# A two-layer decoder trunk on one core: three more weight blocks of the down-projection by seven products instead of eight, and a final norm with its statistics over 512 columns and its instructions in another order

## The chip, the cores and the metric

The kernel runs on one core of one Trainium2 chip. A core has a matrix engine (TensorE: PE in the profile, its weight loads PEld), two engines for element-wise work (VectorE: DVE; ScalarE: ACT), GpSimd (POOL) and SyncE (SP), which here only starts transfers. Each engine works through its own list of instructions in order and waits where an instruction needs what another engine or a transfer has not delivered. The metric is the device time of one execution in microseconds (us); lower is better.

## The reference

A stream `h` of 256 tokens by 2048 channels in float32 goes through two layers. Each ends with the same gated feed-forward part (5504 inner channels) and a layer norm over the channels of every token:

```
u = h @ w_up                                  # 2048 x 11008
c = conv_b + sum_j shift(u, j) * conv_w[j]    # causal, width 3
gate, val = split(c)
ff = (silu(gate) * val) @ w_down              # 5504 x 2048
h = layer_norm(ALPHA * h + ff, ln2_g, ln2_b)  # (x - mean) * rsqrt(var + eps) * g + b
```

Layer 0 mixes tokens by causal pooling before that, layer 1 by three dilated attentions. The output is `h` after the norm of layer 1, the "final norm" of this document.

## The kernel before

**Units.** All the work of TensorE is cut into numbered units, one for a block of weights of up to 512 rows by 512 columns. For every unit the block is loaded (`raw`, three buffers, by SP), split by ACT and DVE, and multiplied. The split keeps float32 accuracy: ACT writes a rounded part `wh` (L99), DVE the rest `wl = raw - wh` (L100), and every product is three matmuls (high by high, high by low, low by high). `wh` and `wl` have four buffers each. `run_units` walks the list: before the matmuls of unit i it issues the loads up to unit i+5 and the split of unit i+3, and behind them what was put off to this unit by `later(n, ...)`. So the order of instructions on every engine is fixed by the order of the units, and each engine keeps to it.

**Down-projection.** Inner channels come in chunks q = 0 to 10 of 512 (the last of 384). A token-major group (`group_tm`) multiplies several chunks with one quarter c of the 2048 output columns. A plain unit has 24 matmuls of 512 columns (L255 to L257). A chunk named in `sevens[q]` for quarter c is done with seven products of quarter blocks in place of eight, which is two units: "a" (18 matmuls of 256 columns) and "b" (24 of them, L244 to L246). Their weights are prepared by `split_sums`: for "a" DVE forms sums inside `raw` (L120, L122, L124) and a low part (L121), for "b" two low parts (L114); the raw buffer is free only after "b". The sums of the left factor are made once for a chunk by `left_sums`. When the last seven-product chunk of a group is done, `early_post` adds what its extra bank pair `s` holds: in layer 1's last groups by five DVE instructions (L845, L846, L853, L855, L857).

**The two places of the change.** In layer 0, chunks 7 and 6 (in that order) make a group for every quarter, which alternate with the up-projection of chunks 9 and 10; chunk 6 goes by sevens in all quarters, chunk 7 in quarters 0 and 1. In layer 1 the last groups are chunks 8, 9, 10 for the four quarters, with chunk 9 by sevens in quarters 0 and 2. The last quarter is done for tokens 0 to 127 first, then for tokens 128 to 255 in two halves of 256 columns (tiles `th`), so that the norm of the first token half (`finish0`) lies under the second half's matmuls; `finish1` norms the second token half after the last matmul.

**Norm.** `tm_post` adds a group's bank to `ht`, the residual in token order, and takes `bn_stats` over every 256 columns. `finish0` and `finish1` aggregate them, take the root on ACT and the reciprocal on DVE. In `finish1` the term `b - mean*rstd*g` of quarters 0 to 2 comes from TensorE: a matmul by the identity adds `b`, and one by a diagonal tile `dg` adds the rest (L936 and L943).

Of the kernel before, what the change touches and what calls it, by code (L numbers as in the profile page):

```python
# [9 lines left out]
F32 = mybir.dt.float32  # L10
F32R = mybir.dt.float32r
I32 = mybir.dt.int32
AF = mybir.ActivationFunctionType
OP = mybir.AluOpType
# [4 lines left out]
P = 128  # L19
# [13 lines left out]
def trunk(ctx: ExitStack, tc: tile.TileContext, x, pool_w_in, pool_w_grp, pool_scale, pool_w_out,  # L33
          attn_w_q, attn_w_o, shared_w_k, shared_w_v, ffn_w_up, ffn_conv_w, ffn_conv_b, ffn_w_down,
          ln1_g, ln1_b, ln2_g, ln2_b, out):
    nc = tc.nc
    V, A, PE = nc.vector, nc.scalar, nc.tensor
# [7 lines left out]
    lnp = ctx.enter_context(tc.tile_pool(name="lnp", bufs=1))  # L45
# [5 lines left out]
    def bank(nm):  # L51
        return pair(nm)[:, 0, :]
# [82 lines left out]
    def later(n, fn):  # L135
        if n == 0:
            fn()
        else:
            pending.append([n, fn])
# [158 lines left out]
    def w4(nm):  # L298
        return lnp.tile([P, 4, T], F32, name=nm, tag="w4")
# [15 lines left out]
    H, XC, XP, ST = {}, {}, {}, {}  # L315
    vec, cvec, gbx = [], [], {}
    ident = const.tile([P, P], F32, name="ident")
# [262 lines left out]
    def ffn(lay):  # L580
# [5 lines left out]
        sevens = {q: every for q in range(8)}  # L586
        sets = {0: "C", 1: "A", 2: "B", 3: "C", 4: "A", 5: "B", 6: "A", 7: "CB"[lay], 9: "A"}
        if lay == 1:
            sevens[9] = (0, 2)
        else:  # L590
            sevens[7] = (0, 1)
        free, done = {}, {}

        def pads():
# [233 lines left out]
    def to_features(c):  # L828
        hb = hp.tile([P, 4, T], F32, name="hb", tag="h")
        hf = hb.rearrange("p m t -> p (m t)")  # L830
        V.transpose(hf.rearrange("p (m t c) -> p t m c", m=4, t=2), HT[c].rearrange("p t (m c) -> p t m c", m=4))

        def to():
            H[c] = hp.tile([P, 4, T], F32, name="h", tag="h")
            return H[c].rearrange("p m t -> p (m t)")

        moves(hf, to)
# [22 lines left out]
    def tm_post(lay, n, c):  # L860
        parts = [slice(0, 256), slice(256, 512)]
        first, last = n == 0, n == 3

        def post(t, ps, half=None):
            y = HT[c][:, t, :]
            if lay == 0 and n == 2 and t == 1:
                later(3, lambda: to_features(c))
            if half is None and first:
                V.scalar_tensor_tensor(y, y, ALPHA, ps, op0=OP.mult, op1=OP.add)
            elif half is None:  # L870
                V.tensor_tensor(y, y, ps, OP.add)
            elif first:
                V.scalar_tensor_tensor(y[:, parts[half]], y[:, parts[half]], ALPHA, ps[:, :256], op0=OP.mult, op1=OP.add)  # L873
                A.activation(y[:, parts[1 - half]], y[:, parts[1 - half]], AF.Copy, scale=ALPHA)
            else:
                V.tensor_tensor(y[:, parts[half]], y[:, parts[half]], ps[:, :256], OP.add)
            if not last:
                return
            if c == 0 and t == 0:
                ST["bn"] = lnp.tile([P, 2, 8, 6], F32, name="bn", tag="bn")  # L880
            for i in range(2) if half is None else (half,):
                V.bn_stats(ST["bn"][:, t, 2 * c + i, :], y[:, parts[i]])
            if c == 2 and t == 1:
                for nm, w in (("g", ln2_g), ("b", ln2_b)):
                    r = rawp.tile([P, 4, 512], F32, name=nm, tag="raw")
                    nc.sync.dma_start(r.rearrange("p a c -> p (a c)"), w[1:2, :].to_broadcast([P, D]))
                    ST[nm] = r
                later(2, early)
            if c == 3 and t == 0:
                finish0()  # L890
            if c == 3 and half == 1:
                finish1()

        def store(by, cc, t, c=slice(0, 512)):
            by.dma_start(out[0, t * P:(t + 1) * P, 512 * cc:512 * cc + 512][:, c], HT[cc][:, t, c])

        def early():
            for t in range(2):
                for cc in range(3):
                    z = HT[cc][:, t, :]  # L900
                    V.tensor_tensor(z, z, ST["g"][:, cc, :], OP.mult)

        def finish0():
            mv = lnp.tile([P, 6], F32, name="mv", tag="mv", bufs=2)
            V.bn_aggr(mv[:, 0:2], ST["bn"][:, 0])
            A.activation(mv[:, 2:3], mv[:, 1:2], AF.Sqrt, bias=epst)
            z = [HT[cc][:, 0, :] for cc in range(4)]
            g, b = [ST["g"][:, cc, :] for cc in range(4)], [ST["b"][:, cc, :] for cc in range(4)]  # L910
            V.scalar_tensor_tensor(z[3], z[3], mv[:, 0:1], g[3], op0=OP.subtract, op1=OP.mult)
            V.reciprocal(mv[:, 3:4], mv[:, 2:3])
            V.scalar_tensor_tensor(mv[:, 4:5], mv[:, 0:1], -1.0, mv[:, 3:4], op0=OP.mult, op1=OP.mult)
            w = lnp.tile([P, 2, 512], F32, name="w", tag="sq")
            for cc in range(2):
                A.activation(z[cc], z[cc], AF.Copy, scale=mv[:, 3:4])
                V.scalar_tensor_tensor(w[:, cc, :], g[cc], mv[:, 4:5], b[cc], op0=OP.mult, op1=OP.add)
                nc.gpsimd.dma_start(z[cc], w[:, cc, :], accum_op=OP.add)
            V.scalar_tensor_tensor(z[3], z[3], mv[:, 3:4], b[3], op0=OP.mult, op1=OP.add)
            store(nc.sync, 3, 0)  # L920
            t = w4("w2")[:, 0:2, :].rearrange("p a n -> p (a n)")
            V.scalar_tensor_tensor(t, g[2], mv[:, 4:5], b[2], op0=OP.mult, op1=OP.add)
            V.scalar_tensor_tensor(z[2], z[2], mv[:, 3:4], t, op0=OP.mult, op1=OP.add)
            for cc in (2, 0, 1):
                store(nc.sync, cc, 0)

        def finish1():
            mv = lnp.tile([P, 6], F32, name="mv", tag="mv", bufs=2)  # L930
            V.bn_aggr(mv[:, 0:2], ST["bn"][:, 1])
            z = [HT[cc][:, 1, :] for cc in range(4)]
            g, b = [ST["g"][:, cc, :] for cc in range(4)], [ST["b"][:, cc, :] for cc in range(4)]
            ps = [bank("gb") for cc in range(3)]
            for cc in range(3):
                PE.matmul(ps[cc], ident, b[cc], start=True, stop=False)  # L936
            A.activation(mv[:, 2:3], mv[:, 1:2], AF.Sqrt, bias=epst)
            V.reciprocal(mv[:, 3:4], mv[:, 2:3])
            V.scalar_tensor_tensor(mv[:, 4:5], mv[:, 0:1], -1.0, mv[:, 3:4], op0=OP.mult, op1=OP.mult)
            dg = w4("dg")[:, 0, :P]  # L940
            V.tensor_scalar(dg, ident, mv[:, 4:5], None, op0=OP.mult)
            for cc in range(3):
                PE.matmul(ps[cc], dg, g[cc], start=False, stop=True)  # L943
            V.scalar_tensor_tensor(z[3], z[3], mv[:, 0:1], g[3], op0=OP.subtract, op1=OP.mult)
            V.scalar_tensor_tensor(z[3], z[3], mv[:, 3:4], b[3], op0=OP.mult, op1=OP.add)
            store(nc.scalar, 3, 1)
            for cc in range(2):
                V.scalar_tensor_tensor(z[cc], z[cc], mv[:, 3:4], ps[cc], op0=OP.mult, op1=OP.add)
                store((nc.sync, nc.scalar)[cc], cc, 1)
            for by, c in zip((nc.sync, nc.scalar), parts):  # L950
                V.scalar_tensor_tensor(z[2][:, c], z[2][:, c], mv[:, 3:4], ps[2][:, c], op0=OP.mult, op1=OP.add)
                store(by, 2, 1, c)
        return post

    ffn(0)
    marks.append(len(units))


    scale = 1.0 / math.sqrt(P)
# [172 lines left out]
    add_last(attn_w_o[0], rows4, [lambda j=j: oq[j] for j in range(4)], True, 1, 0, after=to_tokens)  # L1132
    marks.append(len(units))
    ffn(1)
    marks.append(len(units))

# [34 lines left out]
    with tc.tile_pool(name="pool", bufs=1) as pp:  # L1171
# [5 lines left out]
        for l in range(2):  # L1177
            n = 80 if l == 0 else 64
# [95 lines left out]
```

## Time and profile before

| | |
|---|---|
| median of 3 runs | 2016.1 us (2016.05 to 2018.27) |
| span of the profiled execution | 2014.9 us; its own time is not listed apart from the runs |
| TensorE clock granted | 1.000 over the span |
| HBM read | 380.01 MB, 190 GB/s over the span |
| PE, PEld, DVE, ACT busy | 2005.8, 1810.2, 1734.9, 1269.7 us |

The page sums each engine's busy time over the span. Matmuls are pipelined and their ends are modelled, so a busy PE is not PE at its peak. Two views matter here beside the page: the timeline, with the start and length of each instruction, and the chain of waits, which goes back from the last instruction, at each step to what released it or to the instruction before it on its engine. In the chain "issue" is time in which nothing that the profile shows was waited for, and a name with q (SPq, ACTq) is the engine's sequencer.

### The profile page before, as it was taken

To read this page: it belongs to the slowest core of one execution; us is meant where nothing else is said; L and a number is where in the kernel's file an instruction comes from. 1 tells how busy PE (TensorE), PEld (TensorE's weight loads), DVE (VectorE), ACT (ScalarE), POOL (GpSimd) and SP (SyncE) were. 2 spreads that over 40 slices of the span, in tenths; PEclk is the share of its full clock that TensorE was granted. 3 is DMA by queue.
4 is the path that set the end of the run, shared out by engine and by line. 5 is a ranking of instruction groups with operands and counts; after the bars stand their busy time and mean duration, and the time that the engine had idled before them with its cause. 6 is when DMAs were issued, how large, how long until landed. Compare 5 with 4: busy or idle time off the path is not lost.

```text
span 2014.9 us, 31474 instructions
## 1 busy us (share of the span) xinstructions
PE 2005.8 (100%) x12760; PEld 1810.2 (90%) x12760; DVE 1734.9 (86%) x1831; ACT 1269.7 (63%) x1551; POOL 93.0 (5%) x153
## 2 busy tenths in 40 slices
PE   9999999999999999999999999999999999999999
PEld 8898988999899988889888988998899989989987
DVE  6868887999899899879896878787899899989899
ACT  6454686767766676657554445487766677667673
POOL 2000000000000000000001021000000000000000
PEclk9999999999999999999999999999999999999999
DMA  8565466666666757885465656557666756666765
GB/s 260 204 208 186 163 212 192 181 221 223 198 198 200 239 179 229 232 230 186 155 220 172 210 172 202 187 188 211 166 224 200 224 186 222 209 211 186 213 208 185
DMA packets 271297, 407.77 MB, mean 202 GB/s; under 512 B 74430, under 2 KB 85588, under 8 KB 270896
## 3 DMA queue, kind: packets, MB, share of 16 engines
q1 hardware_dynamic: 259488, 388.93, 58.8%
q0 software_dynamic: 11232, 16.18, 5.4%
q8 instruction: 100, 1.64, 0.3%
q10 hardware_dynamic: 432, 0.66, 0.1%
q14 instruction: 45, 0.37, 0.1%
HBM read 380.01 MB, written 2.10 MB: 190 GB/s over the span
## 4 chain that ended last, share of the span: by engine, by line
PE 88%; DVE 7%; ACT 2%; DMA 2%; issue 1%; SPq 0%; DVEq 0%; ACTq 0%
PE acc L180 41%; PE acc L181 21%; PE s L244 3%; PE s L246 3%; PE s L245 3%; PE acc L184 2%; PE acc L185 2%; PE acc L183 2%; PE t L246 2%; PE t L244 2%; PE t L245 2%; DVE wl L100 2%; ACT wh L99 1%; DVE wl L114 1%; DVE wl L121 1%
## 5 line engine op out<-in xcount | busy, mean ns | idle before, releaser
L180 PE MATMUL acc<-xc,wh 128*128 128x512 f32 x3264 | 1151.6, 396 | 0.0
L181 PE MATMUL acc<-xc,wl 128*128 128x256 f32 x3264 | 916.2, 281 | 0.8 <-DVE wl L100 0.8
L100 DVE TENSOR_TENSOR wl<-raw,wh 128x2048 fp32r<-128x2048 f32 (+2 forms) x304 | 654.8, 2162 | 171.0 <-ACT wh L99 163.3
L180 PEld LDWEIGHTS acc<-xc,wh 128*128 128x128 f32 x3264 | 616.1, 189 | 142.8 <-issue 0.4
L99 ACT CAST wh<-raw 128x2048 fp32r<-128x2048 f32 (+2 forms) x304 | 546.6, 1805 | 170.8 <-PE acc L180 65.7
L181 PEld LDWEIGHTS acc<-xc,wl 128*128 128x128 f32 x3264 | 615.2, 188 | 1.3 <-DVE wl L100 1.2
L113 ACT CAST wh<-raw 128x1024 fp32r<-128x1024 f32 x144 | 150.7, 1052 | 202.8 <-DVE raw L122 175.5
L114 DVE TENSOR_TENSOR wl<-raw,wh 128x1024 fp32r<-128x1024 f32 x144 | 171.8, 1221 | 11.2 <-ACT wh L113 11.2
L121 DVE TENSOR_TENSOR wl<-raw,wh 128x1536 fp32r<-128x1536 f32 x72 | 126.2, 1753 | 6.3 <-ACT wh L119 5.3
L119 ACT CAST wh<-raw 128x1536 fp32r<-128x1536 f32 x72 | 106.4, 1477 | 36.6 <-PE acc L180 26.5
L287 POOL DMA_DIRECT2D ht<-w x48 | 41.3, 1015 | 1446.4 <-DVE ht L873 720.9
L244 PE MATMUL t<-wh,g 128*128 128x256 f32 x376 | 105.8, 281 | 0.0
L246 PE MATMUL t<-wh,g 128*128 128x256 f32 x376 | 105.7, 281 | 0.0
L245 PE MATMUL t<-wl,g 128*128 128x256 f32 x376 | 105.5, 281 | 0.0
L616 ACT ACTIVATE c<-u,cv 128x256 f32<-128x256 f32 x172 | 89.5, 593 | 23.2 <-DVE f L678 16.5
L246 PE MATMUL s<-wh,xs 128*128 128x256 f32 x344 | 96.1, 279 | 0.0
L244 PE MATMUL s<-wh,xs 128*128 128x256 f32 x344 | 95.9, 279 | 0.0
L245 PE MATMUL s<-wl,xs 128*128 128x256 f32 x344 | 95.9, 279 | 0.0
L124 DVE TENSOR_TENSOR raw<-raw 128x1024 f32<-128x1024 f32 x72 | 88.2, 1225 | 2.4
L621 ACT ACTIVATE a<-u,cv 128x256 f32<-128x256 f32 x172 | 73.5, 500 | 11.9 <-DVE g L688 11.9
L607 ACT COPY u<-acc 128x512 f32<-128x512 f32 x84 | 46.8, 572 | 46.1 <-PE acc L181 45.9
L621 ACT ACTIVATE u<-u,cv 128x256 f32<-128x256 f32 x172 | 73.4, 500 | 0.0
(338 smaller groups left out, 3443.1 us busy)
## 6 DMA issues: line engine op xcount, KB each, us to landing
raw<-in_ffn_w_up_dram SPq DMA_DIRECT2D x160, 1024.0 KB, 5.2
raw<-in_ffn_w_down_dram SPq DMA_DIRECT2D x80, 1024.0 KB, 5.1
raw<-in_pool_w_out_dram SPq DMA_DIRECT2D x16, 1024.0 KB, 5.0
raw<-in_shared_w_k_dram SPq DMA_DIRECT2D x16, 1024.0 KB, 5.2
raw<-in_attn_w_q_dram SPq DMA_DIRECT2D x16, 1024.0 KB, 5.3
raw<-in_shared_w_v_dram SPq DMA_DIRECT2D x16, 1024.0 KB, 5.4
raw<-in_attn_w_o_dram SPq DMA_DIRECT2D x16, 1024.0 KB, 5.2
ht<-w POOLq DMA_DIRECT2D x50, 256.0 KB, 4.8
```

The lines of the kernel that those rows point to most:

```text
L99: A.copy(wh[i][:, s], r[:, s])
L100: V.tensor_tensor(wl[i][:, s], r[:, s], wh[i][:, s].bitcast(F32), OP.subtract)
L113: A.copy(h[:, :, n], r[:, :, n])
L114: V.tensor_tensor(l[:, :, n], r[:, :, n], h[:, :, n].bitcast(F32), OP.subtract)
L119: A.copy(hs, rs)
L121: V.tensor_tensor(ls, rs, hs.bitcast(F32), OP.subtract)
L180: PE.matmul(ps[m].ap, h[:, k, c], q[:, k, :, :T], start=st, stop=False)
L181: PE.matmul(ps[m][:, :T], l[:, k, c], q[:, k, 0, :T], start=False, stop=sp)
L244: PE.matmul(to, xh, h[:, k, n], start=opens and kk == 0, stop=False)
L245: PE.matmul(to, xh, l[:, k, n], start=False, stop=False)
L246: PE.matmul(to, xl, h[:, k, n], start=False, stop=ends and kk == 1)
L621: A.activation(to[:, m, :], u[:, m, i:i + T], AF.Copy, scale=cv[:, i, j:j + 1])
```

## The change

- `sevens`: in layer 0 chunk 7 goes by seven products in all four quarters (quarters 2 and 3 are new); in layer 1 chunk 9 in quarters 0, 1 and 2 (1 is new). Where all four quarters of a chunk go by sevens, `left_sums` puts the fourth sum into unused columns of the chunk's own tile instead of the tiles `xs3S` and `xs3Q`.
- Statistics are taken over 512 columns where the whole row is there; the halves of the last quarter of the second token half stay apart. The tile `bn` and the aggregations shrink with it.
- The last part of `finish0` (quarter 2 and three stores) becomes `rest`, which is called after the statistics of the first half of the last quarter.
- In `finish1` half of the centring of quarter 3 stands ahead of the reciprocal, and `dg` is made by ACT.

The short description of the change also speaks of low parts of sums in halves; the diff has no further edit of that kind.

```diff
@@ ffn
         sevens = {q: every for q in range(8)}
         sets = {0: "C", 1: "A", 2: "B", 3: "C", 4: "A", 5: "B", 6: "A", 7: "CB"[lay], 9: "A"}
         if lay == 1:
-            sevens[9] = (0, 2)
-        else:
-            sevens[7] = (0, 1)
+            sevens[9] = (0, 1, 2)
@@ tm_post
-                ST["bn"] = lnp.tile([P, 2, 8, 6], F32, name="bn", tag="bn")
-            for i in range(2) if half is None else (half,):
-                V.bn_stats(ST["bn"][:, t, 2 * c + i, :], y[:, parts[i]])
+                ST["bn"] = lnp.tile([P, 2, 5, 6], F32, name="bn", tag="bn")
+            if half is None:
+                V.bn_stats(ST["bn"][:, t, c, :], y)
+            else:
+                V.bn_stats(ST["bn"][:, t, 3 + half, :], y[:, parts[half]])
...
             if c == 3 and t == 0:
-                finish0()
+                ST["rest"] = finish0()
+            if c == 3 and half == 0:
+                ST["rest"]()
@@ finish0
-            V.bn_aggr(mv[:, 0:2], ST["bn"][:, 0])
+            V.bn_aggr(mv[:, 0:2], ST["bn"][:, 0, :4])
...
             store(nc.sync, 3, 0)
-            t = w4("w2")[:, 0:2, :].rearrange("p a n -> p (a n)")
-            V.scalar_tensor_tensor(t, g[2], mv[:, 4:5], b[2], op0=OP.mult, op1=OP.add)
-            V.scalar_tensor_tensor(z[2], z[2], mv[:, 3:4], t, op0=OP.mult, op1=OP.add)
-            for cc in (2, 0, 1):
-                store(nc.sync, cc, 0)
+            def rest():
+                t = w4("w2")[:, 0:2, :].rearrange("p a n -> p (a n)")
+                V.scalar_tensor_tensor(t, g[2], mv[:, 4:5], b[2], op0=OP.mult, op1=OP.add)
+                V.scalar_tensor_tensor(z[2], z[2], mv[:, 3:4], t, op0=OP.mult, op1=OP.add)
+                for cc in (2, 0, 1):
+                    store(nc.sync, cc, 0)
+            return rest
@@ finish1
             A.activation(mv[:, 2:3], mv[:, 1:2], AF.Sqrt, bias=epst)
+            def centred(c):
+                V.scalar_tensor_tensor(z[3][:, c], z[3][:, c], mv[:, 0:1], g[3][:, c], op0=OP.subtract, op1=OP.mult)
+            centred(parts[0])
             V.reciprocal(mv[:, 3:4], mv[:, 2:3])
             V.scalar_tensor_tensor(mv[:, 4:5], mv[:, 0:1], -1.0, mv[:, 3:4], op0=OP.mult, op1=OP.mult)
             dg = w4("dg")[:, 0, :P]
-            V.tensor_scalar(dg, ident, mv[:, 4:5], None, op0=OP.mult)
+            A.activation(dg, ident, AF.Copy, scale=mv[:, 4:5])
             for cc in range(3):
                 PE.matmul(ps[cc], dg, g[cc], start=False, stop=True)
-            V.scalar_tensor_tensor(z[3], z[3], mv[:, 0:1], g[3], op0=OP.subtract, op1=OP.mult)
+            centred(parts[1])
```

What this moves is seen in the order of the built programs (names carry buffer numbers; sizes are partitions by elements of the output). First DVE in layer 1's last groups, from the last low part of the gate product (L305) on; `w` and `s` are `early_post` of quarter 0, the last row the split of chunk 8 in quarter 2. Before:

```order
L305 TENSOR_TENSOR g<-c,g 128x3x256
L100 TENSOR_TENSOR wl_18401<-raw_18325,wh_18400 128x2048
L845 TENSOR_TENSOR w<-w,s 128x256
L846 TENSOR_TENSOR w<-w,s 128x256
L853 TENSOR_TENSOR ht<-ht,w 128x512
L855 TENSOR_TENSOR ht<-ht,w 128x512
L857 TENSOR_TENSOR ht<-ht,s 128x2x256
L100 TENSOR_TENSOR wl_18438<-raw_18371,wh_18437 128x1536
L100 TENSOR_TENSOR wl_18467<-raw_18398,wh_18466 128x2048
```

Where one split of chunk 9 for quarter 1 stood, six instructions stand now, four ahead of `early_post` and two behind it, in the same place of the changed kernel:

```order
L305 TENSOR_TENSOR g<-c,g 128x3x256
L120 TENSOR_TENSOR raw_18377<-raw_18377 128x2x256
L121 TENSOR_TENSOR wl_18451<-raw_18377,wh_18450 128x2x768
L122 TENSOR_TENSOR raw_18377<-raw_18377 128x2x256
L124 TENSOR_TENSOR raw_18377<-raw_18377 128x4x256
L843 TENSOR_TENSOR w<-w,s 128x256
L844 TENSOR_TENSOR w<-w,s 128x256
L851 TENSOR_TENSOR ht<-ht,w 128x512
L853 TENSOR_TENSOR ht<-ht,w 128x512
L855 TENSOR_TENSOR ht<-ht,s 128x2x256
L114 TENSOR_TENSOR wl_18491<-raw_18377,wh_18490 128x4x256 x2
L100 TENSOR_TENSOR wl_18525<-raw_18448,wh_18524 128x1536
```

A second `early_post`, that of quarter 1, follows some ten rows later, ahead of the last two low parts of quarter 2; before, none stood there:

```order
L120 TENSOR_TENSOR raw_18522<-raw_18522 128x2x256
L121 TENSOR_TENSOR wl_18576<-raw_18522,wh_18575 128x2x768
L122 TENSOR_TENSOR raw_18522<-raw_18522 128x2x256
L124 TENSOR_TENSOR raw_18522<-raw_18522 128x4x256
L843 TENSOR_TENSOR w<-w,s 128x256
L844 TENSOR_TENSOR w<-w,s 128x256
L851 TENSOR_TENSOR ht<-ht,w 128x512
L853 TENSOR_TENSOR ht<-ht,w 128x512
L855 TENSOR_TENSOR ht<-ht,s 128x2x256
L114 TENSOR_TENSOR wl_18616<-raw_18522,wh_18615 128x4x256 x2
```

So the last low parts of quarter 2 now stand five instructions further back.

The third place is ACT in layer 0, from the split of chunk 7 for quarter 3 to the weights of the value half of chunk 10 (`c<-u,cv` is a step of the convolution). Before:

```order
L99 CAST wh_7888<-raw_7811 128x2048
L119 CAST wh_7918<-raw_7856 128x2x768
L113 CAST wh_7953<-raw_7856 128x4x256 x2
L607 COPY u<-acc 128x2x256
L607 COPY u<-acc 128x256
L99 CAST wh_7998<-raw_7916 128x1536
L616 ACTIVATE c<-u,cv_583 128x256 x3
```

The same place in the changed kernel:

```order
L119 CAST wh_7913<-raw_7842 128x2x768
L113 CAST wh_7944<-raw_7842 128x4x256 x2
L119 CAST wh_7978<-raw_7911 128x2x768
L605 COPY u<-acc 128x2x256
L605 COPY u<-acc 128x256
L113 CAST wh_8024<-raw_7911 128x4x256 x2
L614 ACTIVATE c<-u,cv_583 128x256 x3
L99 CAST wh_8061<-raw_7976 128x1536
```

The rounded parts for "b" of chunk 6 have moved behind the two copies, and the cast for the first value unit behind the three convolution steps.

## The prediction, made before the changed kernel was run

> **What bounds the kernel now.** I read the page first, then the chain of waits, then the busy time in stretches.
>
> ```profile
> span 2014.9 us, 31474 instructions
> PE 2005.8 (100%) x12760; PEld 1810.2 (90%) x12760; DVE 1734.9 (86%) x1831; ACT 1269.7 (63%) x1551; POOL 93.0 (5%) x153
> PE 88%; DVE 7%; ACT 2%; DMA 2%; issue 1%; SPq 0%; DVEq 0%; ACTq 0%
> ```
>
> Over the whole span PE carries the chain, with 88% of it, and has next to no idle time. The chain is not the same everywhere, though. Layer 1's last groups, where the third new unit lies, read so, engine by engine:
>
> ```profile
> core 0: us, PE busy (x) PEld busy (x) DVE busy (x) ACT busy (x) POOL busy (x), PEclk, DMA share, GB/s
> 1960.00:1985.00 25.00, 25.00 (x130) 21.09 (x129) 24.58 (x28) 12.14 (x10) 0.00 (x0) 1.00 0.62 209
> 1985.00:2005.00 20.00, 20.00 (x120) 17.65 (x120) 19.29 (x32) 5.04 (x7) 1.72 (x2) 1.00 0.41 144
> ```
>
> DVE is busy for 24.58 of 25.00 us and then 19.29 of 20.00. It has no room left there, and the chain of waits of the same place runs through it:
>
> ```profile
> 1960.13 0.06 DVE wl L100
> ...
> 1962.34 0.42 DVE w L845
> ...
> 1965.05 1.19 DVE wl L100
> ...
> 1969.00 0.61 DVE ht L871
> ...
> 1969.63 0.75 DVE bn L882 x2
> ...
> 1971.76 0.59 DVE raw L120
> ...
> 1976.01 2.36 DVE wl L114 x2
> 1978.37 0.02 issue
> 1978.38 4.93 DMA raw<-in_ffn_w_down_dram
> ...
> 1983.42 1.92 ACT wh L99
> ...
> 1985.36 2.29 DVE wl L100
> ...
> 2003.35 0.68 DVE w L922
> ...
> 2004.80 0.34 DVE ht L876
> ...
> 2005.60 0.33 DVE ht L876
> ...
> 2006.41 0.38 DVE mv L931
> ```
>
> From 1960.13 to 2006.41 it is DVE after DVE, with one load (of chunk 9 for the last quarter, whose raw buffer is free only at 1978.37) in between; DVE worked on other things meanwhile. PE is no wait in it: its last product for the tokens ends where the row below starts, and DVE begins the first of the two last additions at 2004.80, the second at 2005.60.
>
> ```profile
> 2004.75 0.59 PE L936 MATMUL gb<-b,ident 128*128 128x512 f32 x1
> ```
>
> So PE and DVE arrive at the end together, and in these 45 us a microsecond taken from PE is worth nothing unless DVE is relieved too, while one laid on DVE is paid in full.
>
> **PE's gain.** Four PE rows of layer 0, the first matmul of the pair of chunks 7 and 6 and the first behind it, for quarter 1 (both by sevens) and quarter 2 (chunk 7 plain):
>
> ```profile
> 773.58 0.28 PE L244 MATMUL s<-wh,g 128*128 128x256 f32 x1
> ...
> 783.39 0.39 PE L180 MATMUL acc<-xc,wh 128*128 128x512 f32 x1
> ...
> 805.88 0.40 PE L255 MATMUL t<-wh,g 128*128 128x512 f32 x1
> ...
> 816.41 0.39 PE L180 MATMUL acc<-xc,wh 128*128 128x512 f32 x1
> ```
>
> With chunk 7 plain the pair takes 816.41 - 805.88 = 10.53 us, by sevens 783.39 - 773.58 = 9.81. A unit by sevens saves 0.72 us of PE, three 2.2.
> [...]
>
> **DVE's price of one such unit.** In the chain, "a" takes 1971.76 to 1976.01 and "b" to 1978.37: 6.61 us. The plain split it replaces takes 1960.13 to 1962.34: 2.21. That is 4.40 us more DVE per unit. In layer 1, quarter 1 gets its own `early_post` too, five instructions, as quarter 0's from 1962.34 to 1965.05: 2.71.
>
> **Layer 0, two units.** PE gains 1.44. DVE gets 8.80 more and spares two half-width additions (0.61 - 0.34 each). What covers that:
>
> ```profile
> 813.21 1.76 DVE L100 TENSOR_TENSOR wl<-raw,wh 128x1536 fp32r<-128x1536 f32 x1 [3.38 <-DMA h<-hb]
> 832.26 2.32 DVE L114 TENSOR_TENSOR wl<-raw,wh 128x1024 fp32r<-128x1024 f32 x2
> 840.98 0.28 PE L244 MATMUL s<-wh,xs 128*128 128x256 f32 x1
> ```
>
> For quarter 2 the idle 3.38 us ahead of 813.21 take most of the 4.40. Some 1.0 us of backlog, less 0.27 for quarter 2's addition, goes on to quarter 3, which brings its own 4.40. There, chunk 6's "b" parts end at 832.26 + 2.32 = 834.58 and PE wants them at 840.98: 6.4 us of slack. In the changed kernel PE comes 1.44 earlier and DVE some 5.1 later, so the slack is -0.2, about zero; PE can start on the first of the two low parts, and I take a stall of 0.3 for what this sum leaves open. Behind it ACT's order counts: the cast for the next unit stands behind the two "b" casts and three convolution steps, where it stood ahead of the steps, and I take 0.5 for that. Net for layer 0: -1.44 + 0.8 = -0.6, bounds -1.4 (no stall) and +1.0 (a backlog of 2.4 us, all of it stalled). The loads that follow wait longer for their raw buffers (chunk 7's is held until its "b" is split), and SP's queue puts one load behind eleven small `h<-hb` transfers. The slack of a load here is about the three units of its look-ahead, so I cost that at nothing; if it is late, ACT's cast is the next to wait. The gain reaches the end, because after this stage the chain is PE's until layer 1's end.
>
> **Layer 1, one unit.** DVE: +4.40 + 2.71 = 7.1. PE's 0.72 less is worth nothing, since DVE ends last. DVE's first new instruction needs only the raw block, not ACT's cast that ended at 1960.1, so it starts some 0.15 earlier. Nothing stands between to absorb the rest: DVE's only wait (for the load above, then ACT's 1.92) moves along, since that load starts when quarter 2's "b" is split, before and after. PE in its turn has to wait. With the changed list laid out on these durations, it waits some 1.2 us for "b" of quarter 1, 0.6 for chunk 8 and 0.6 for "b" of quarter 2, and 2.6 for chunk 10 behind the second `early_post`: 5.0 in all. It ends 5.0 - 0.7 = 4.3 later than before, DVE's last addition comes some 6.5 later, so the products then lie there about 3 us before DVE asks for them.
>
> **Statistics.** Two rows of 256 take 0.75 together. One over 512 is not in the trace. Nearest are additions: 0.61 at 512 against 0.34 at 256, so 512 costs 0.07 less than twice 256. I take 0.68 for 0.75. Seven such pairs change (both token halves of quarters 0 to 2, one of quarter 3); those of quarter 1 lie ahead of the wait for the load and only lengthen it. Five count: 0.35, and 0.05 for the smaller aggregation. Bounds: 0 (as two halves) to 5 x 0.34 = 1.7 (a 512 as cheap as a 256). A pair dearer than now is excluded by the additions.
>
> **`rest` moved.** The same instructions (0.68 and 0.75) stand between the two halves' additions instead of ahead of both. DVE comes late to both halves, so the sum stays: nothing. Were DVE early, they would fill its wait for the second half, up to 1.4. SP's three stores go out later, but two of them wait for POOL's additions anyway and none is last.
>
> **`finish1`.**
>
> ```profile
> 2006.82 0.30 ACT mv L937
> ...
> 2007.15 0.17 DVE mv L938
> ...
> 2007.54 0.30 DVE dg L941
> ...
> 2007.88 2.86 PE gb L943 x6
> ...
> 2010.76 0.48 DVE ht L951
> ```
>
> After the aggregation DVE waits 0.35 us for the root; half a centring (0.48 by the last row, 256 columns with the same form) goes there and pushes the reciprocal back by 0.05 to 0.15. `dg` by ACT instead of DVE: its nearest rows are the root at one column, 0.30, and this of the page, at 256:
>
> ```profile
> L621 ACT ACTIVATE a<-u,cv 128x256 f32<-128x256 f32 x172 | 73.5, 500 | 11.9 <-DVE g L688 11.9
> ```
>
> For 128 columns I take 0.40 where DVE took 0.30. What DVE saves behind it, half a centring and `dg`, lies under the 2.86 us of PE that decide when the last rows start. So +0.15, bounds 0 and +0.4.
>
> **Sum** against the profiled execution: 2014.9 - 0.6 (layer 0) + 7.1 - 0.15 - 0.4 (layer 1 and statistics) + 0.15 (`finish1`) = 2021.0. The median of the runs, 2016.1, lies 1.2 over the span; I take that as constant: 2022.2, or +0.30%. Anything within 0.2% (4.0 us) can't be told from no change.
>
> **Rivals.**
>
> A: *PE decides.* By the page, PE and its weight loads (100% and 90%) stand over DVE's 86%. If DVE's work in the last groups can slip behind PE's, each unit gives its 0.72, -2.2, and `rest` fills a gap, up to 0.4 more: 2016.1 - 2.6 = 2013.5, not slower. It decides if DVE has at least 7 us of slack there; the 24.58 of 25.00 speaks against it, and the chain, in which no PE row stands between 1960.13 and 2007.88.
> [...]
>
> B: *The gains all go to their good ends:* no stall in layer 0 (-1.4) and a 512-column statistic as cheap as a 256 one (-1.7), against 7.1 - 0.15 - 0.05 (aggregation) + 0.15 (`finish1`): +3.95, so 2020.1, at the edge of no change.
>
> C: *Backlog in layer 0.* DVE's and ACT's lists there were near full, and if ACT's cast comes later than I worked out, quarters 2 and 3 stall for 2.5 us and more together: +1.0 in place of -0.6, and another microsecond of waits for raw buffers: 2022.2 + 2.6 = 2024.8. It speaks for it that the slack is about zero by my sum, against it that quarters 0 and 1 run the same sequence without loss, though between longer units.
>
> That the change does not do what it says is excluded by the order of the built programs, which holds the new units, the single statistics and the moved `rest`.
>
> **How the numbers follow.** My forecast 0.64 (its own range 2020.4 to 2024), C 0.10, B or something like it 0.11, A 0.11, and 0.04 for something else that makes it faster by a way I don't see. Forecast and C are slower by over 0.2%, save a tenth of the forecast at its lower edge: 0.68. A, B and the rest of the forecast's edge lie within: 0.28. Faster by over 0.2% would need -4.0, more than all gains that I find together: the 0.04. The range leaves out A and the last of C: 2017.5 to 2024.5.
>
> **What the profile of the changed kernel would show.** PE: quarters 2 and 3 of layer 0 at about 9.8 and 10.6 us instead of 10.53, with a wait on DVE or ACT at the second. In the last groups, waits of PE for `wl` (L114 and L100) of 1 to 3 us each, which were none before; DVE without a gap; the aggregation of `finish1` 6 us later against PE's arrival in layer 1's last groups. A statistic over 512 columns at 0.6 to 0.7 us a piece. `dg` by ACT at about 0.4. I am wrong if PE shows no such waits, or if DVE turns out to have idle time between 1960 and the end.

## The result, and the profile after

The changed kernel takes 2026.58 us (median of 5 runs, 2024.44 to 2030.28), the kernel before 2017.74 us beside it: a ratio of 1.0051 with a 95% interval [1.0040, 1.0062], some 10 us slower (the two medians are 8.8 us apart, within that interval). The forecast was 2022.2 with a range up to 2024.5. Single executions of one kernel lie several us apart here, so what follows rests on such ratios with their intervals, and profiles are read for places, not for totals. The profiled execution took 2024.44 us, at a span of 2022.7.

The page of the changed kernel, its span, engines and chain:

```profile
span 2022.7 us, 31610 instructions
PE 2006.8 (99%) x12814; PEld 1812.5 (90%) x12814; DVE 1748.9 (86%) x1844; ACT 1275.5 (63%) x1559; POOL 93.1 (5%) x153
PE 46%; DVE 8%; ACT 2%; DMA 2%; issue 1%; POOL 0%; SPq 0%; DVEq 0%; ACTq 0%; POOLq 0%
```

PE's busy time is about that of before (2005.8), DVE's is 14 us more. Busy time by engine in layer 1's last groups (columns as in the prediction):

```profile
1961.00:1986.00 25.00, 24.73 (x140) 21.13 (x139) 24.66 (x29) 12.76 (x12) 0.00 (x0) 1.00 0.45 158
1986.00:2013.00 27.00, 24.77 (x139) 21.18 (x139) 26.00 (x37) 6.57 (x7) 1.72 (x2) 0.94 0.46 156
```

DVE is as full as it was (24.66 of 25.00, then 26.00 of 27.00), PE has gaps now, and the granted clock is 0.94 in the second stretch. The chain of waits of the changed kernel at the same place, from the first new instruction to the last norm:

```profile
1961.38 0.60 DVE raw L120
...
1965.55 0.42 DVE w L843
...
1969.39 1.22 DVE wl L114
...
1981.37 0.34 DVE w L843
...
1990.67 6.05 DMA raw<-in_ffn_w_down_dram
...
2014.16 0.30 DVE mv L937
...
2014.48 0.48 DVE ht L946
...
2015.33 0.41 ACT dg L952
...
2015.79 2.86 PE gb L954 x6
```

The sums of the new unit (L120 to L114) and two `early_post` (L843, at 1965.55 and 1981.37) stand in the chain of DVE, and the last aggregation comes at 2014.16 in place of 2006.41. From the first instruction of the new unit it is 2014.16 - 1961.38 = 52.78 us; before, from the split that it replaces, 2006.41 - 1960.13 = 46.28: +6.50. Of the span's 7.8 us, 1.25 are there already when DVE enters these groups (1961.38 against 1960.13).

Those come from layer 0, behind which PE stays about 3 us late (3.17 at the matmul below, 2.97 at 1955). The first matmul of layer 0's norm, before and after, is the plainest sign of it (timeline of PE; in brackets the idle time ahead of the instruction and what ended it):

```profile
887.36 0.28 PE L384 MATMUL shift<-S,ones 128*128 128x256 f32 x1
```

```profile
890.53 0.36 PE L384 MATMUL shift<-S,ones 128*128 128x256 f32 x1 [2.61 <-DVE S L367]
```

It is 3.17 us late, and 2.61 of it are a wait for DVE that the kernel before does not have. In the profiles of four kernels run below that leave layer 0's units as they were, this matmul lies between 0.14 us early and 0.51 late, so single profiles can be read here to about half a us. I had forecast PE 0.6 us early there. What makes DVE late begins some 50 us earlier. Here is the timeline of SP's queue before, and then of the changed kernel (raw blocks by L89, small transfers `h<-hb` between them):

```profile
824.75 2.57 SPq L89 DMA_DIRECT2D raw<-in_ffn_w_up_dram  x2
832.37 3.86 SPq L821 DMA_DIRECT2D h<-hb  x6
836.32 0.55 SPq L89 DMA_DIRECT2D raw<-in_ffn_w_up_dram  x1
836.91 3.20 SPq L821 DMA_DIRECT2D h<-hb  x5
840.21 0.56 SPq L89 DMA_DIRECT2D raw<-in_ffn_w_up_dram  x1
```

```profile
825.00 0.37 SPq L89 DMA_DIRECT2D raw<-in_ffn_w_up_dram  x1
833.66 3.86 SPq L819 DMA_DIRECT2D h<-hb  x6
837.62 0.55 SPq L89 DMA_DIRECT2D raw<-in_ffn_w_up_dram  x1
838.21 3.20 SPq L819 DMA_DIRECT2D h<-hb  x5
841.50 0.55 SPq L89 DMA_DIRECT2D raw<-in_ffn_w_up_dram  x1
842.09 4.22 SPq L819 DMA_DIRECT2D h<-hb  x5
846.41 0.55 SPq L89 DMA_DIRECT2D raw<-in_ffn_w_up_dram  x1
```

Before, two up-projection blocks go out ahead of the first six small transfers, in the changed kernel one; the second leaves at 837.62 instead of about 827, the third at 841.50 instead of 836.32, the fourth at 846.41 instead of 840.21. The look-ahead of `run_units` counts units, and a plain unit that becomes "a" and "b" is two: the same number of units ahead now reaches one block less far, while the small transfers stay where they were.

The queue is not the whole of it: a load also waits for its raw buffer. The third block takes the buffer of chunk 6 in quarter 3, which is free when DVE has made the last low part for "b": 832.26 + 2.32 = 834.58 before, and in the changed kernel the last row of that work ends at 839.85 + 1.22 = 841.07 (timeline of DVE):

```profile
839.85 1.22 DVE L114 TENSOR_TENSOR wl<-raw,wh 128x1024 fp32r<-128x1024 f32 x1
```

So the queue holds the third block for 0.43 us only. The second, whose buffer is free at 832.47, it holds for 5.15, but no engine waits for that one. For the third block ACT does wait, where it did not before (timeline of ACT, before and after):

```profile
841.69 1.47 ACT L99 CAST wh<-raw 128x1536 fp32r<-128x1536 f32 x1
```

```profile
847.62 1.48 ACT L99 CAST wh<-raw 128x1536 fp32r<-128x1536 f32 x1 [2.03 <-DMA raw<-in_ffn_w_up_dram]
```

and DVE's list goes back with it (timeline of DVE, before and after):

```profile
844.87 1.22 DVE L305 TENSOR_TENSOR g<-c,g 128x1024 fp32r<-128x1024 f32 x1
...
885.23 0.42 DVE L367 TENSOR_TENSOR S<-fold 128x256 fp32r<-128x256 f32 x1
```

```profile
850.80 1.22 DVE L305 TENSOR_TENSOR g<-c,g 128x1024 fp32r<-128x1024 f32 x1
...
889.96 0.42 DVE L367 TENSOR_TENSOR S<-fold 128x256 fp32r<-128x256 f32 x1
```

The gate product is 5.93 us late, as is ACT's cast, and the sum `S` 4.73, and for `S` PE waits.

### The profile page after: what moved, and what is told of

It reads as the page before. It is cut to its first block, busy times and chain, and to the rows that moved or that the text cites. A ratio compares the mean times of both kernels' runs of the same rounds, so it can differ in the third digit from the quotient of the medians.

```text
span 2022.7 us, 31610 instructions
## 1 busy us (share of the span) xinstructions
PE 2006.8 (99%) x12814; PEld 1812.5 (90%) x12814; DVE 1748.9 (86%) x1844; ACT 1275.5 (63%) x1559; POOL 93.1 (5%) x153
## 4 chain that ended last, share of the span: by engine, by line
PE 46%; DVE 8%; ACT 2%; DMA 2%; issue 1%; POOL 0%; SPq 0%; DVEq 0%; ACTq 0%; POOLq 0%
PE acc L180 21%; PE acc L181 11%; DVE wl L100 2%; PE s L246 2%; PE s L244 2%; PE s L245 2%; PE t L246 1%; PE t L245 1%; PE t L244 1%; ACT wh L99 1%; PE acc L184 1%; PE acc L185 1%; PE acc L183 1%; DMA raw<-in_ffn_w_down_dram 1%; DVE wl L121 1%
## 5 line engine op out<-in xcount | busy, mean ns | idle before, releaser
L100 DVE TENSOR_TENSOR wl<-raw,wh 128x2048 fp32r<-128x2048 f32 (+2 forms) x301 | 647.9, 2160 | 162.8 <-ACT wh L99 161.4
L99 ACT CAST wh<-raw 128x2048 fp32r<-128x2048 f32 (+2 forms) x301 | 540.8, 1804 | 167.1 <-PE acc L180 66.7
L113 ACT CAST wh<-raw 128x1024 fp32r<-128x1024 f32 x150 | 156.8, 1052 | 206.6 <-DVE raw L122 186.9
L114 DVE TENSOR_TENSOR wl<-raw,wh 128x1024 fp32r<-128x1024 f32 x150 | 179.0, 1221 | 11.3 <-ACT wh L113 11.3
L121 DVE TENSOR_TENSOR wl<-raw,wh 128x1536 fp32r<-128x1536 f32 x75 | 131.4, 1752 | 7.2 <-ACT wh L119 6.0
L246 PE MATMUL t<-wh,g 128*128 128x256 f32 x396 | 111.4, 281 | 0.0
L244 PE MATMUL t<-wh,g 128*128 128x256 f32 x396 | 111.3, 281 | 0.0
L245 PE MATMUL t<-wl,g 128*128 128x256 f32 x396 | 111.2, 281 | 0.0
L245 PE MATMUL s<-wl,xs 128*128 128x256 f32 x362 | 101.0, 279 | 0.3 <-DVE wl L114 0.3
L246 PE MATMUL s<-wh,xs 128*128 128x256 f32 x362 | 101.0, 279 | 0.0
L244 PE MATMUL s<-wh,xs 128*128 128x256 f32 x362 | 100.9, 279 | 0.0
L245 PEld LDWEIGHTS t<-wl,g 128*128 128x128 f32 x396 | 74.7, 189 | 0.0
```

Of the source, the lines that this page charges most:

```text
L99: A.copy(wh[i][:, s], r[:, s])
L100: V.tensor_tensor(wl[i][:, s], r[:, s], wh[i][:, s].bitcast(F32), OP.subtract)
L113: A.copy(h[:, :, n], r[:, :, n])
L114: V.tensor_tensor(l[:, :, n], r[:, :, n], h[:, :, n].bitcast(F32), OP.subtract)
L121: V.tensor_tensor(ls, rs, hs.bitcast(F32), OP.subtract)
L244: PE.matmul(to, xh, h[:, k, n], start=opens and kk == 0, stop=False)
```

## The experiments

**The parts alone.** Each part of the change was put into the kernel before by itself. Layer 0:

```diff
-        else:
-            sevens[7] = (0, 1)
```

> Layer 0's two units alone. The prediction's step: -0.6 us against before. The account from the trace of the changed kernel: the loads of the last up-projection weights go out behind the small h transfers, the load ring then runs late, PE waits 2.5 to 3 us at the shift matmul near 888 us, and some 1.8 us of that is caught up before layer 1's last groups: +1 to +1.6 us at the end. [...]

1.0020 [1.0011, 1.0028], 2020.48 against 2016.62: 4.0 us slower. The theory with the cost in layer 0 holds, though it cost more than the 1 to 1.6 us expected; my own term of -0.6 does not. Layer 1:

```diff
-            sevens[9] = (0, 2)
+            sevens[9] = (0, 1, 2)
```

> Layer 1's unit alone (chunk 9 by sevens in quarters 0, 1, 2). If DVE decides in the last groups: +6.8 to +7.1 us of span (4.40 for the split, 2.71 for early_post, none of the statistics' saving), with a wait of PE of 2.5 us or more for the low part of chunk 10 in quarter 2, and half-clock stretches behind it, so runs spread by some us. If PE decides: -0.7 us.

1.0039 [1.0026, 1.0052], +7.9 us where 6.8 to 7.1 were expected; the last aggregation comes at 2014.12, 7.7 us after that of the kernel before. The norm (everything else in the diff):

> The norm alone (statistics over 512 columns, rest, half centring, dg by ACT), weight units as before. With 0.60 us in place of 0.75 per pair, five of seven pairs on the way: about -0.6 us; aggregations -0.15; finish1 +0.15: -0.4 to -0.7 us. The prediction's step: -0.25. If the norm's part were free of effect: 0.

0.9999 [0.9990, 1.0008]: nothing that can be told. In its profile the chain of the last groups is PE's, so what the norm spares on DVE shortens nothing there. The parts add to 4.0 + 7.9 - 0.2 = 11.7 us; together they cost 10.3. That PE's lateness from layer 0 in part lies under DVE's longer chain in layer 1 (of its 2.97 us at 1955 only 1.25 are seen where DVE enters) would explain the difference, which is no larger than the intervals.

**What in layer 1.** The new unit without the `early_post` of its quarter, which leaves that quarter's extra sums out of the result:

```diff
+            if c == 1 and not by_dma:
+                return
```

> Layer 1's unit alone, with early_post of quarter 1 left out: its five DVE instructions and one ACT copy are not issued and what its bank pair holds is not added. If DVE decides: 2.71 us less than with it, +5.0 us against before (+4.5 to +5.3). If PE decides: the same as with it, +7.7.

1.0027 [1.0018, 1.0037], 2021.63. The aggregation comes at 2011.89, 2.23 us ahead of that with the five instructions. Counted from the first new instruction (1959.79 with them, 1960.29 without) to the aggregation it is 54.33 and 51.60 us, where it was 46.28. So the five instructions cost 2.73, and their rows take 2.71. The split costs 5.32, more than the 4.40 of its rows. The rest is a wait that the prediction did not have: DVE stands 0.80 us (0.90 with the five instructions) before "a" of quarter 2, for a load that goes out only when "b" of quarter 1 frees its raw buffer. In the chain of waits of layer 1's unit alone:

```profile
1967.81 1.23 DVE wl L114
...
1969.06 6.55 DMA raw<-in_ffn_w_down_dram
...
1975.71 1.49 ACT wh L119
...
1977.22 1.77 DVE wl L121
```

Both pieces of DVE's work are paid in full, each separately: that is shown. The wait is not in the profile of the whole changed kernel, where the same count is 52.78 with the statistics' saving in it. The profiled execution without the five instructions shows one thing more (chain of waits, and granted clock in a stretch):

```profile
2013.36 5.50 PE gb L945 x6
```

```profile
2013.00:2018.50 5.50, 5.14 (x6) 1.85 (x6) 3.19 (x5) 0.00 (x0) 0.00 (x0) 0.50 0.65 225
```

The same six matmuls that take 2.86 us above take 5.50 at a granted clock of 0.50.

**What in layer 0.** First the order on SP: with the two units, the loads of the units around the change go out one unit earlier, which restores what stood ahead of the small transfers.

```diff
-        while state["loaded"] < min(len(units), i + LD_AHEAD + 1):
+        while state["loaded"] < min(len(units), i + LD_AHEAD + 1 + (172 <= i < 190)):
```

> Layer 0's two units, with loads issued one unit earlier between units 172 and 189, so that each goes out ahead of the same h transfers as in the kernel before. If the queue's order is what made the load ring late: the wait at the shift matmul goes, and the time is -0.5 to -1.4 us against before. If DVE's and ACT's backlog alone made it: +1 to +1.6 us as without it.

1.0010 [1.0001, 1.0019]: half of the loss is gone by the ratios, whose intervals overlap, and PE's wait at the shift matmul is 1.9 in place of 2.6. Neither expectation fits. In its profile two blocks stand ahead of the first small transfers again, but the third leaves only at 840.69, and the gate product is still 4.23 us late. One of the two units alone:

```diff
-            sevens[7] = (0, 1)
+            sevens[7] = (0, 1, 2)
```

> Layer 0 with chunk 7 by sevens in quarters 0, 1 and 2, so one new unit, in quarter 2, ahead of which DVE had 3.4 us of idle time. If the loss in layer 0 comes from the backlog that quarter 3 hands on: no wait at the shift matmul beyond that of before, and -0.7 us (-1 to 0). If any new unit there upsets the load ring: +1 us or more, with a wait of 1 us or more at the shift matmul.

1.0011 [1.0002, 1.0019]: with the first unit about half of the loss is there, and in its profile a wait of 1.3 us at the shift matmul. So it is not only the second unit's lack of slack, on which the prediction had spent its care. The same with the norm:

> The norm's part and the one unit of layer 0 in quarter 2, none of the others: the two parts that should not cost. -0.7 (unit) - 0.2 (norm): -0.9 us (-1.3 to 0). If the unit in quarter 2 upsets the load ring: +1 us.

1.0008 [0.9999, 1.0017]; no gain.

**The clock.** In the profile of layer 0's units alone the granted clock halves behind the wait. Three us of that kernel, and the same three of the kernel before:

```profile
893.50:896.50 3.00, 3.00 (x11) 2.52 (x11) 2.88 (x3) 0.39 (x1) 1.90 (x2) 0.50 0.67 125
```

```profile
893.50:896.50 3.00, 3.00 (x19) 2.63 (x18) 2.73 (x5) 3.00 (x6) 0.00 (x0) 1.00 1.19 207
```

11 matmuls instead of 19 in the same 3 us: PE is 4.38 us late at the shift matmul and 6.00 behind that stretch. To see whether this is the loss, twelve matmuls by the identity were put ahead of the shift matmul, so that PE is busy while it waits:

```diff
+        if not first and lay == 0:
+            for i in range(12):
+                PE.matmul(ps[:, :P], ident, ident, start=True, stop=True)
```

> Layer 0's two units, and twelve matmuls of the identity by itself (some 2.4 us by the transposes' 0.2 us each) written to the shift bank right ahead of the shift matmul, where PE waited 2.9 us. If a half-clock stretch of 3.41 us follows PE's waiting and costs time: the clock stays at 1.000 there, the jump of 1.6 us behind the shift matmul goes, and the time is +0.5 to +1.5 us against before, with runs closer together. If the stretch costs nothing, or has nothing to do with the waiting: +3.5 to +4 us as without the filling, and more if the filling itself delays the shift matmul.

1.0035 [1.0022, 1.0049], slower than without the filling, though the clock is 1.000 in four of five runs. In the profile no half-clock stretch follows (granted clock 1.000), and the shift matmul is 2.15 us late all the same. The filling itself hardly holds it up: `S` ends at 889.21 there and the matmul starts at 889.52. Keeping the clock up does not bring the time back; the stretch was a price on top, not the cause. What the filled kernel loses beyond that lies elsewhere. A second profile of it:

> The kernel with layer 0's two units and 12 fillers ahead of the shift matmul once more, for a profile of one of its longer executions (22 to 24 us over 2000 at a granted clock of 1.0, in three of five). Theory 1 (a load lands late somewhere behind layer 0, in single executions): the PE offset against before is about +2.2 at the shift matmul as in the first profile and jumps by 3 to 6 us at one later wait on a DMA. Theory 2 (the loss in layer 0 itself varies): the offset at the shift matmul is already 5 to 8 us. If the execution is a short one (span below 2019), it tells nothing.

2025.39 us, span 2023.6, clock 1.000. At the shift matmul PE is 3.35 us late, between the two theories; the rest comes later, in five waits of this kind (waits of PE from there to 1860):

```profile
PE acc L181 <- DVE wl L100: 5.0, 5, 1.7
```

PE loses 1.2 us between 1500 and 1860 in the first profile of the filled kernel and 5.9 in the second; where those late steps begin, in which load, I did not find. The two units alone, once more:

> Layer 0's two units alone once more, for a second profile. Theory 1 (the length of the wait for the shift matmul varies little, 4.4 us in the first profile, and the half-clock stretch behind it comes or does not come): offset at the shift matmul 3.5 to 5, and the end offset is 0 to 1 us more without the stretch and 1.5 more with it. Theory 2 (the loss in layer 0 itself varies from execution to execution, between 0 and 8 us): the offset at the shift matmul differs from 4.4 by more than 1.5.

2019.78 us. The shift matmul is 2.12 us late, 2.3 less than in the first profile, so the loss in layer 0 does vary from execution to execution, and a half-clock stretch follows again (granted clock 0.50 from 890.00 to 893.00, PE 3.72 late behind it). Both theories had a part of it.

Where the two executions part can be seen. The load of chunk 7 for quarter 3 lands 9.2 us after its issue in the first (at 826.23) and 7.5 in the second (824.35). DVE begins the sums of that chunk at 826.25 and 824.93, and PE waits 1.66 and 0.56 us for the last low part for "b" of chunk 6 in quarter 3 (at 841.44 and 840.07). Behind this the two are 1.36 us apart, of the 2.26 at the shift matmul. In the changed kernel the load took 7.9 us, and PE did not wait there.

**The cause in layer 0.** If the blocks are late because they stand behind small transfers, it should help to take those off the queue. The two units, with `h<-hb` issued by POOL:

```diff
-    def moves(fr, to):
+    def moves(fr, to, by=nc.sync):
...
-                nc.sync.dma_start(dst[0][32 * b:32 * b + 32, a], fr[32 * a:32 * a + 32, b])
+                by.dma_start(dst[0][32 * b:32 * b + 32, a], fr[32 * a:32 * a + 32, b])
...
-        moves(hf, to)
+        moves(hf, to, nc.gpsimd)
```

> Layer 0's two units alone, and the 64 transfers h<-hb of the kernel (32 KB each) go by POOL's queue in place of SP's, where they stood between the loads. Theory 1 (the loads go out late behind these transfers on SP's queue, half of the loss): as with the loads one unit earlier, about +2 us against before, the shift matmul of layer 0 (887.36 in before) late by 1 to 1.5 us in place of 4.4. Theory 2 (the raw buffers come free late, so that the order of SP does not matter): +4 as in the run with the two units alone, the shift matmul late by 4. Theory 3 (POOL's own transfers are slower to issue, so that h comes late to the convolution): later than +4, with waits on DMA h<-hb.

1.0002 [0.9993, 1.0011], 2017.52 against 2016.85. The loss is gone within the noise, which is more than theory 1 had expected. Its loads and its shift matmul (timelines of SP and PE):

```profile
824.45 0.37 SPq L89 DMA_DIRECT2D raw<-in_ffn_w_up_dram  x1
831.05 0.37 SPq L89 DMA_DIRECT2D raw<-in_ffn_w_up_dram  x1
840.00 0.37 SPq L89 DMA_DIRECT2D raw<-in_ffn_w_up_dram  x1
842.53 0.37 SPq L89 DMA_DIRECT2D raw<-in_ffn_w_up_dram  x1
```

```profile
887.04 0.36 PE L384 MATMUL shift<-S,ones 128*128 128x256 f32 x1 [0.89 <-DVE S L367]
```

The second block leaves at 831.05 instead of the changed kernel's 837.62, the fourth at 842.53 instead of 846.41, and PE waits 0.89 us. The third still leaves at 840.00: there it waits for its raw buffer and not for the queue. The gate product is therefore still 4.02 us late, but `S` only 1.24, where it was 4.73: without the transfers the lateness is caught up on the way. The control, the kernel before with the same move:

> The kernel before with only the transfers h<-hb on POOL's queue in place of SP's, as a control for the run above. Theory 1: these transfers are slack in the kernel before, PE decides there: within 0.5 us of before. Rival: POOL issues 64 transfers more slowly than SP and h comes late: +1 us or more, with PE or DVE waiting on h<-hb behind 805 us.

1.0004 [0.9995, 1.0013]: for the kernel before these transfers make no difference. So it is the two together, shown by the runs with neither, either and both: the units are harmless without the transfers on the queue, and the transfers are harmless without the units. By which way the transfers do it is not shown. They hold loads back on the queue, and without them the loads issued from 820 to 862 land 5.5 us after their issue in the median, where it was 7.1 in the changed kernel (5.2 and 7.9 for that of chunk 7 in quarter 3; the longest 9.9 and 8.3); these two were not tried apart.

**Together.** The whole change with the transfers on POOL's queue, and the same without layer 1's unit:

> The whole changed kernel with only the transfers h<-hb on POOL's queue in place of SP's. Theory 1 (the miss of the prediction is these transfers ahead of layer 0's loads, and what is left is layer 1's unit on DVE): 2016.9 + 7.9 - 0.3 = 2024.5 at the most and 2022 at the least; against the changed kernel as it is 2 to 4 us less, the shift matmul of layer 0 within 0.7 us of before in place of 3.2 late. Theory 2 (the parts do not add, so that layer 1's waiting covers what layer 0 wins): within 1 us of the changed kernel as it is, 2026.

> The changed kernel without layer 1's new unit (chunk 9 by sevens in quarters 0 and 2, as before), and with the transfers h<-hb on POOL's queue: the best version that the runs point to. Theory 1: layer 0's two units at no loss (ratio 1.0002 alone) and the norm's -0.2 us: 2016.5 to 2017, the same as before, since what PE gains by the two units is waited for again at the shift matmul. Theory 2 (the gain of 1.4 us of PE reaches the end once the loads are in time): 2015.3, 1.5 us faster.

The first takes 1.0034 [1.0021, 1.0048], about 2024 on the scale of theory 1, between its ends, and some 3.5 us less than the changed kernel as it is (1.0051; the intervals overlap a little). Its shift matmul is not within 0.7 us, though:

```profile
889.13 0.36 PE L384 MATMUL shift<-S,ones 128*128 128x256 f32 x1 [1.80 <-DVE S L367]
```

1.77 us late, with a half-clock stretch behind it: the next matmuls of 512 columns take 0.58 and 0.63 us, where those ahead of it take 0.40 and those in the changed kernel's stretch at 1991.72 take 0.63. The second is 1.0001 [0.9992, 1.0010], theory 1's "the same as before", with the same wait of 1.8 us. No version with these units that was run is faster than the kernel before; in the profiles PE waits at the shift matmul for about what the two units gain.

## Why the prediction was right or wrong

**What bounds the kernel** was read rightly: the last groups belong to DVE, and both pieces of DVE work put there cost at least their rows' time. DVE has no gap above 0.55 us there in the changed kernel.

**Layer 1** was right in size: 7.1 - 0.4 = 6.7 in the sum from the new unit's start to the aggregation, 6.50 measured. That it comes so near is in part luck: alone, the unit costs 8.05 by the same count, with DVE's wait of 0.90 for a load that the prediction left out. PE's products for the norm start later by 2011.82 - 2004.75 = 7.07 us, 2.97 of it brought along from layer 0, so 4.1 for the 4.3 worked out; but the waits lie otherwise than I had laid them out. PE's waits in the changed kernel, from 1955 to 2016:

```profile
PE t L256 <- DVE wl L100: 2.2, 1, 2.2
...
PE s L245 <- DVE wl L114: 0.3, 1, 0.3
```

The one for chunk 10 is there (2.6 forecast), and of the 0.6 for "b" of quarter 2 half; those of 1.2 for "b" of quarter 1 and 0.6 for chunk 8 are not. The waits add to 2.5 us for the 5.0 forecast, and the half-clock stretch behind the wait for chunk 10 adds some 1.6: that PE's lateness agrees is luck.

**Statistics and `finish1`** were about right and too small to matter. All 512-wide statistics of the changed kernel, by line:

```profile
L880 DVE BATCH_NORM_STATS2 bn<-ht 128x6 f32<-128x512 f32 x7 | 4.9, 695 | 0.2
```

0.70 where I took 0.68. `dg` by ACT takes 0.41 (0.40 taken), and from the aggregation to the products it is 2015.79 - 2014.16 = 1.63 us where it was 2007.88 - 2006.41 = 1.47: +0.16 for +0.15. `rest` cost nothing that shows.

**Layer 0** is the step that failed: -0.6 forecast, +4.0 measured. In the changed kernel's profile it is not the stall I worked out: the pairs of quarters 2 and 3 take 9.90 and 10.05 us (about 9.8 and 10.6 forecast), a wait of 0.45 follows (I had taken 0.5 for ACT's order), and at the start of the last groups of layer 0, behind both new units, PE was 0.31 us early. With layer 0's units alone the stall at "b" of quarter 3 is there too, 1.66 and 0.56 us in two profiles where I took 0.3, so that term was too small in some executions. What failed above all is the sentence after it: that a load's slack was "about the three units of its look-ahead, so I cost that at nothing". I had seen the block behind eleven small transfers and the buffers held longer, and named ACT's cast as next to wait; I did not work out that a look-ahead of units is a shorter one when a unit is split in two, nor that the third block's buffer comes free 6.49 us later (841.07 for 834.58), nor follow a block that leaves 5.18 us late through cast, DVE and the shift matmul some 50 us on. Taking the transfers off the queue gives back (1.0020 - 1.0002) x 2016.9 = 3.6 of the 4.0 us.

**Rival C** was nearest (2024.8, with a backlog of DVE and ACT in layer 0). Its stalls of 2.5 us in quarters 2 and 3 did not come in the changed kernel; its "another microsecond of waits for raw buffers" points at the part that did, though not at the transfers. A is out by layer 1 alone (+7.9). B is out by the statistics, 0.70 us a piece over 512 columns where B had them at the 0.42 of 256, and by layer 0.

**Time over span.** I added 1.2 us, the median of the runs over a span of another execution. Time less span is about 1.8 us in every run listed here with both. The forecast span of 2021.0 stands against 2022.7 in the profile, 1.7 us off; the rest of the miss of 4.4 is that 0.6 and a median 2.1 us above the profiled execution.

**What stays open**: how much of the loss in layer 0 is the order on the queue and how much the later landing; why one load lands 7.5 us after its issue in one execution and 9.2 in another; why two kernels with the transfers moved still wait 1.8 us at the shift matmul and a third 0.9; and where the filled kernel's later steps in layer 1 come from. More raw buffers would test how much of the rest is the buffers' part; that was not tried.

## What to carry to other kernels

Where loads are issued a fixed number of steps ahead, a change that splits a step shortens the look-ahead for everything behind it: list what each queue holds ahead of each load and when the load's buffer comes free, before and after, and follow the first late load to the engine that ends the stage. Where small transfers stand between large loads, another queue for them is worth a run: here it gave back 3.6 us in one kernel and nothing in another. A saving on the engine that carries the chain is worth working out only after the fuller neighbours have been asked, stage by stage, whether they can keep up.

## What the runs showed of the hardware

The half-clock stretch of the changed kernel was 3.41 us long: the granted clock is 0.50 from 1991.69 to 1995.10, behind a wait of 2.23 us. It is 0.50 as well over 893.50 to 896.50 in layer 0's units alone, 890.00 to 893.00 in their second profile and 1991.50 to 1994.50 in layer 1's unit alone, and over 2013.00 to 2018.50 at the end of layer 1's unit without the five instructions of `early_post`, so that this last stretch was at least 5.50 us long. In layer 0 such a stretch put PE back by about 1.6 us (4.38 to 6.00, 2.12 to 3.72, 1.77 to 3.38 us late at layer 0's norm). At 1991.69 in the changed kernel, where DVE carries the chain, no row of PE stands in the chain around it, and it cost nothing that the chain shows. In layer 0 a stretch began behind waits of 1.80 us (the changed kernel with the transfers moved), 2.14 and 2.61 us (layer 0's units alone, second and first profile), and did not come behind one of 1.8 us (the changed kernel with the transfers moved and without layer 1's unit, granted clock 1.000) nor behind one of 2.61, that of the changed kernel at 890.53 (1.00 from 891.00 to 896.50). So the length of the wait alone does not tell whether a stretch comes; what does is not shown by these runs.
